# A chunked state-space scan: each step handed to the order of the program in three pieces instead of two

## The chip, the cores and the metric

The kernel runs on one core of a Trainium2 chip. The metric is the device time of one execution in microseconds (us), lower is better. The engines are named as in the profile: PE (TensorE, matrix products), PEld (its weight loads), DVE (VectorE), ACT (ScalarE), POOL (GpSimd) and SP (SyncE, which issues most DMAs). Each engine works through its own instructions strictly in order, and semaphores make it wait for others.

## The reference, cut to what matters

One layer of a streaming encoder for 16 meta tokens and 512 frames, width 1024. The token mixer has two branches, both scans over chunks of 64 frames; a second part (PEER) chooses experts for each token and costs most of the time. The change lies in the second scan, of the SSD branch. Its 32 heads form four groups of eight; the chunk step of the reference, for all groups, is:

```python
def ssd_chunk_step(S, inp):
    xdt, a, Bc, Cc = inp
    acum = jnp.cumsum(a, axis=1)
    seg = jnp.exp(-jnp.abs(acum[:, :, None] - acum[:, None, :]))
    cb = jnp.einsum('btgn,bsgn->btsg', Cc, Bc)
    y = jnp.einsum('btsgr,btsg,bsgrp->btgrp', seg, cb, xdt)
    y = y + jnp.einsum('btgn,bgrpn,btgr->btgrp', Cc, S, jnp.exp(acum))
    to_end = jnp.exp(acum[:, -1:] - acum)
    S = S * jnp.exp(acum[:, -1])[..., None, None] + jnp.einsum('bsgn,bsgr,bsgrp->bgrpn', Bc, to_end, xdt)
    return S, y
```

After the scan y is gated with silu(z), normalised by group, and goes into an up projection. x, B, C and z come from projections of the normed input; x, B and C also pass a convolution over time of four taps.

## The kernel before, in words

The scan is done group by group (0 to 3) by the generator `sscan(g)` (lines 339 to 452). One step i (0 to 3) covers 128 frames, that is two chunks, whose states are sA (before the first) and sB (between the two). A `yield` in a generator gives control back to `drive` (line 53), which has several generators run in turn: it always lets the one run next that is least far on by the weight it was given.

Beside the scan of group g runs `sproj(g+1)`, the projections of the next group, in ten units: two for B and C (`conv`: 48 matmuls into pa and pb, copies rw on ACT, three taps cv on DVE, a silu that ends in BT or CT), four for x (the same, ending in xT, with the transposes px and pxm of an earlier block in two of them and in the two units that follow), and four for z (24 matmuls into pk each). Beside the scan of group 3 run ten units of `gates` (24 matmuls into pq each, then gr), six more gates units follow it, and `lows` (tiles zr, zh), which is placed by the scheduler as early as the scan of group 0. Each unit's weights come by a DMA from SP (raw), are rounded on ACT (whi) and the remainder is formed on DVE (wlo).

After a prologue, a step of the scan has two pieces:

- the pointwise piece: DVE multiplies sgm (the decays between frames) by cb; POOL forms xw, the decayed state sB, sgm times dt, the spread R of the step after (lines 379 to 384), and xd;
- the product piece: ACT normalises the y of the step before; PE does the chunk sums ssp for both states, the diagonal products py from sgm, the transposes pyt of the step before; DVE adds ssp to sB, and py to xd. Then PE does C with the states, pi (lines 435 and 436: the first half of the rows from sA, the second from sB), DVE makes y from pi, xd and z, ACT squares and sums it (into xd and sy), POOL makes ry, and `decays` (lines 386 to 394) starts sgm of the next step: two matmuls pr, a subtraction on DVE, two ACT passes (abs and exp).

The generators give the program order alone. What stands in each engine's queue is decided by a scheduler on top of it, by priority and free buffers, so an instruction can stand earlier than its piece (xw and xd of steps 0 and 1, R of step 2 and later do). The buffers that matter: two of xd, xw and R, three of y and of the weights' raw, whi and wlo, four PSUM banks that ssp, py, pyt, pi, pr, px and pxm share.

Of the kernel before, what the change touches and what calls it, by code (L numbers as in the profile page):

```python
# [40 lines left out]
NGT = 6  # L41
# [15 lines left out]
def drive(*parts):  # L57

    live = [[0, n, g] for n, g in parts]
    while live:  # L60
        p = min(live, key=lambda x: (x[0] + 1) / x[1])
        p[0] += 1
        if next(p[2], StopIteration) is StopIteration:
            live.remove(p)
# [12 lines left out]
def body(tc, a, out):  # L77
# [3 lines left out]
    def act(o, i, f, **kw):  # L81
        S.activation(out=o, in_=i, func=f, **kw)  # L82
# [9 lines left out]
    with ExitStack() as top:  # L92
# [9 lines left out]
        def mps(name):  # L102
            return ps.tile([128, 512], F32, name=name, tag="m")
# [91 lines left out]
        def hv(x, c):  # L195
            return x.rearrange("p (h c) -> p h c", c=c)

        with ExitStack() as mix:
# [140 lines left out]
            def sscan(g):  # L339
# [30 lines left out]
                def turn(i, y):  # L370
                    p = mps("pyt")
                    for h in range(4):
                        T.transpose(p[:, 128 * h:128 * h + 128], y[:, 128 * h:128 * h + 128], ident)
                    yt = sg.tile([128, 512], F32, name="yt", bufs=2)
                    act(yt, p, AF.Copy)
                    nc.sync.dma_start(yT_d[:, 4 * g:4 * g + 4, 128 * i:128 * i + 128], hv(yt, 128))
# [30 lines left out]
                for i in range(TT):  # L407
                    s8 = hv(sgm, 64)
                    tt(V, s8, s8, cb[:, i][:, None, :].to_broadcast([128, 8, 64]), OP.mult)
                    xw = sg.tile([128, 512], F32, name="xw", bufs=2)  # L410
                    tt(G, hv(xw, 64), hv(xs[:, i], 64), bc(tdt[:, i + 1], g), OP.mult)
                    sB = decay(ex[:, i, 64:96], sA)
                    tt(G, s8, s8, bc(dt[:, i + 1], g), OP.mult)
                    if i < 3:
                        R = spread(i + 1)
                    xd = sg.tile([128, 512], F32, name="xd", bufs=2)
                    tt(G, hv(xd, 64), hv(xs[:, i], 64), bc(dsk, g), OP.mult)
                    yield
                    if yp:
                        norm(*yp[1:])  # L420
                    pB = spsum(bt[:, i], xw, slice(0, 64))
                    pA = spsum(bt[:, i], xw, slice(64, 128)) if i < 3 else None
                    tt(V, sB, sB, pB, OP.add)
                    py = mps("py")
                    for h in range(8):
                        cs = slice(64 * h, 64 * h + 64)
                        for c in range(2):
                            rw = slice(64 * c, 64 * c + 64)
                            T.matmul(py[rw, cs], sgm[rw, cs], xs[rw, i, cs], start=True, stop=True)
                    tt(V, xd, xd, py, OP.add)  # L430
                    if yp:
                        turn(*yp[:2])
                    t0 = NM + 128 * i
                    pi = mps("pi")
                    T.matmul(pi[0:64], CT[:, t0:t0 + 64], sA, start=True, stop=True)
                    T.matmul(pi[64:128], CT[:, t0 + 64:t0 + 128], sB, start=True, stop=True)
                    if i < 3:
                        sA = decay(ex[:, i, 96:128], sB)
                        tt(V, sA, sA, pA, OP.add)
                    y = sg.tile([128, 512], F32, name="y", bufs=3)  # L440
                    tt(V, hv(y, 64), hv(pi, 64), bc(ex[:, i], g), OP.mult)
                    tt(V, y, y, xd, OP.add)
                    tt(V, y, y, zt[:, i], OP.mult)
                    sy = sg.tile([128, 1], F32, name="sy")
                    act(xd, y, AF.Square, accum_out=sy)
                    if i < 3:
                        sgm = decays(i + 1, R)
                    yp = (i, y, rstd(sg, sy, 1, 512, "ry", 4 * EPS))
                    yield
# [3 lines left out]
            def gates(n0, n1, pool, nb):  # L453
                for b in range(n0, n1):
                    (p, _, _), = tproj(a["wgate"][b], 1)
                    gr = pool.tile([128, 512], F32, name="gr", tag="t", bufs=nb)
                    act(gr, p, AF.Tanh, scale=0.5)
                    nc.sync.dma_start(ga_d[:, b], gr)
                    yield
# [256 lines left out]
            sg = mix3.enter_context(tc.tile_pool(name="sg", bufs=3))  # L716
# [6 lines left out]
            for g in range(3):  # L723
                s_ = sscan(g)
                next(s_)
                drive((9, s_), (10, sproj(g + 1)))
            s_ = sscan(3)
            next(s_)
            drive((9, s_), (16 - NGT, gates(0, 16 - NGT, sg, 2)),
                  (2 * (NQ + NL - NE) + 5, lows(NE, NQ + NL, lambda n: sg.tile([128, 512], F32, name="zr", bufs=5),  # L730
                                                lambda n: sg.tile([128, 512], F32R, name="zh", bufs=3), S)))
            mix3.close()
# [505 lines left out]
```

## Time and profile before

| | us |
|---|---|
| three runs, median (lowest to highest) | 2148.63 (2145.14 to 2150.17) |
| the profiled execution, its own time | 2149.09 |
| its span, first to last instruction | 2147.3 |
| PE busy | 2071.9 |
| DVE busy | 1537.4 |
| ACT busy | 919.7 |
| POOL busy | 594.0 |

The second scan lies between 330 and 662 us. Groups 0 to 3 begin at 330.5, 417.2, 501.2 and 585.0 us, where the products pcb of each stand. A matmul's end is modelled in these records, so the distance from start to start says more than its duration; a wait that the page puts down to a releaser stands in square brackets.

### The profile page before, as it was taken

To read this page: it belongs to the slowest core of one execution; us is meant where nothing else is said; L and a number is where in the kernel's file an instruction comes from. 1 tells how busy PE (TensorE), PEld (TensorE's weight loads), DVE (VectorE), ACT (ScalarE), POOL (GpSimd) and SP (SyncE) were. 2 spreads that over 40 slices of the span, in tenths; PEclk is the share of its full clock that TensorE was granted. 3 is DMA by queue.
4 is the path that set the end of the run, shared out by engine and by line. 5 is a ranking of instruction groups with operands and counts; after the bars stand their busy time and mean duration, and the time that the engine had idled before them with its cause. 6 is when DMAs were issued, how large, how long until landed. Compare 5 with 4: busy or idle time off the path is not lost.

```text
span 2147.3 us, 33001 instructions
## 1 busy us (share of the span) xinstructions
PE 2071.9 (96%) x12458; PEld 1824.6 (85%) x12458; DVE 1537.4 (72%) x2695; ACT 919.7 (43%) x1468; POOL 594.0 (28%) x536
## 2 busy tenths in 40 slices
PE   5999999999999999989998999999999999999998
PEld 4787777877777989979997989899899989898997
DVE  6543568576653668988998666777777687777776
ACT  6642345554434454444465433333333333333332
POOL 5430224344340000000000004443434444334432
PEclk9899999999999999999999999999999999999999
DMA  8842235222236787679565898899889888988884
GB/s 291 301 163 69 75 106 169 75 69 79 89 104 221 256 269 240 232 260 321 198 247 230 316 295 281 300 316 310 304 311 320 278 325 307 324 301 309 302 303 182
DMA packets 200223, 507.16 MB, mean 236 GB/s; under 512 B 16720, under 2 KB 89040, under 8 KB 198400
## 3 DMA queue, kind: packets, MB, share of 16 engines
q1 hardware_dynamic: 149440, 312.10, 43.1%
q0 software_dynamic: 46592, 185.62, 23.9%
q10 hardware_dynamic: 4032, 7.34, 1.0%
q8 instruction: 97, 1.59, 0.3%
q14 instruction: 62, 0.51, 0.1%
HBM read 448.38 MB, written 56.62 MB: 235 GB/s over the span
## 4 chain that ended last, share of the span: by engine, by line
PE 79%; DVE 7%; issue 5%; DMA 4%; ACT 4%; POOL 1%; SPq 0%; POOLq 0%; ACTq 0%; DVEq 0%
PE va L1111 24%; PE pA L88 7%; PE pA L90 7%; PE pA L89 7%; PE pk L90 3%; PE pk L88 3%; PE pk L89 3%; PE pya L88 2%; PE pya L89 2%; PE pq L254 2%; PE pya L90 2%; PE pq L255 2%; PE pq L257 2%; DVE cv L293 1%; ACT whi L82 1%
## 5 line engine op out<-in xcount | busy, mean ns | idle before, releaser
L82 ACT ACTIVATE whi<-raw 128x1024 fp32r<-128x1024 f32 x433 | 458.4, 1059 | 552.0 <-PE pA L89 297.2
L85 DVE TENSOR_TENSOR wlo<-raw,whi 128x1024 fp32r<-128x1024 f32 x385 | 473.1, 1230 | 202.6 <-ACT whi L82 200.0
L88 PE MATMUL pA<-hh,whi 128*128 128x384 f32 x1024 | 348.4, 340 | 6.8 <-ACT ga L970 4.8
L90 PE MATMUL pA<-hh,wlo 128*128 128x384 f32 x1024 | 347.3, 339 | 1.9 <-DVE wlo L85 1.9
L89 PE MATMUL pA<-hl,whi 128*128 128x384 f32 x1024 | 346.6, 339 | 0.0
L1050 POOL DMA_INDIRECT u<-in_pu,ix x128 | 175.0, 1367 | 323.9 <-ACT gh L1098 279.8
L1050 POOL DMA_INDIRECT u<-in_pv,ix x128 | 168.4, 1315 | 255.9 <-ACT gh L1098 210.0
L1111 PE MATMUL va<-whi,gh 128*128 128x512 f32 x768 | 237.6, 391 | 0.3 <-ACT whi L82 0.3
L1111 PE MATMUL va<-wlo,gh 128*128 128x512 f32 x768 | 237.1, 390 | 0.5 <-DVE wlo L85 0.5
L1064 DVE SCALAR_TENSOR_TENSOR hacc<-u,acg,hacc 128x1024 f32<-128x1024 f32 x128 | 164.5, 1285 | 98.2 <-DMA u<-in_pv,ix 97.3
L1058 DVE SCALAR_TENSOR_TENSOR scr<-u,hg 128x1024 f32<-128x1024 f32 x128 | 156.6, 1223 | 109.1 <-DMA u<-in_pu,ix 108.8
L88 PEld LDWEIGHTS pA<-hh,whi 128*128 128x128 f32 x1024 | 193.4, 189 | 10.9 <-ACT ga L970 5.1
L89 PEld LDWEIGHTS pA<-hl,whi 128*128 128x128 f32 x1024 | 193.9, 189 | 4.1
L1098 ACT ACTIVATE gh<-ga 128x384 fp32r<-128x384 f32 x128 | 67.1, 525 | 303.8 <-PE va L1111 286.2
L90 PEld LDWEIGHTS pA<-hh,wlo 128*128 128x128 f32 x1024 | 193.2, 189 | 2.7 <-DVE wlo L85 2.6
L1111 PEld LDWEIGHTS va<-wlo,gh 128*128 128x128 f32 x768 | 144.2, 188 | 31.5 <-DVE wlo L85 1.0
L1111 PEld LDWEIGHTS va<-whi,gh 128*128 128x128 f32 x768 | 142.8, 188 | 23.1 <-ACT whi L82 0.6
L88 PE MATMUL pya<-oyh,whi 128*128 128x256 f32 x384 | 107.7, 280 | 1.0 <-ACT whi L82 1.0
L89 PE MATMUL pya<-oyl,whi 128*128 128x256 f32 x384 | 107.4, 280 | 0.0
L90 PE MATMUL pya<-oyh,wlo 128*128 128x256 f32 x384 | 107.3, 279 | 0.0
L88 PE MATMUL pk<-whi,hh 128*128 128x512 f32 x256 | 103.0, 402 | 0.0
L90 PE MATMUL pk<-whi,hl 128*128 128x512 f32 x256 | 101.7, 397 | 0.0
(925 smaller groups left out, 4469.1 us busy)
## 6 DMA issues: line engine op xcount, KB each, us to landing
raw<-in_puT SPq DMA_DIRECT2D x128, 512.0 KB, 5.0
raw<-in_pv SPq DMA_DIRECT2D x128, 512.0 KB, 5.3
raw<-in_wup SPq DMA_DIRECT2D x48, 512.0 KB, 4.3
wlo<-lo_d SPq DMA_DIRECT2D x48, 512.0 KB, 4.9
W_d<-stg POOLq DMA_DIRECT2D x12, 2048.0 KB, 9.1
wb<-W_d SPq DMA_DIRECT2D x32, 768.0 KB, 7.7
raw<-in_wpq SPq DMA_DIRECT2D x32, 512.0 KB, 5.4
raw<-in_wxbc SPq DMA_DIRECT2D x24, 512.0 KB, 3.4
```

The lines of the kernel that those rows point to most:

```text
L82: S.activation(out=o, in_=i, func=f, **kw)
L85: eng.tensor_tensor(o, x, y, op=op)
L88: T.matmul(o, lh, rh, start=first, stop=False)
L89: T.matmul(o, lh, rl, start=False, stop=False)
L90: T.matmul(o, ll, rh, start=False, stop=last)
L254: T.matmul(p[:, :n], h[:, k], hh[:, k, sl], start=k == 0, stop=False)
L255: T.matmul(p[:, :n], h[:, k], hl[:, k, sl], start=False, stop=False)
L1050: g_ = G.indirect_dma_start(out=u, out_offset=None, in_=a[tab], in_offset=bass.IndirectOffsetOnAxis(ap=ix[:, i, k:k + 1], axis=0))
L1058: V.scalar_tensor_tensor(scr, u, 1.0, hg[:, i], op0=OP.mult, op1=OP.mult, accum_out=ac_[:, k:k + 1])
L1064: V.scalar_tensor_tensor(hacc[:, i], u, ac_[:, k:k + 1], hacc[:, i], op0=OP.mult, op1=OP.add)
L1098: i = S.activation(out=gh, in_=ga, func=AF.Copy)
L1111: T.matmul(va[t][c], x[:, cs], y[:, 512 * c:512 * c + 512], start=st_, stop=en_)
```

## The change

The product piece gets a `yield` of its own between the transposes of the step before and the product of C with the states. So a step has three pieces, called A (pointwise), B (states and diagonal products) and C (the product with C and all that follows from it), and the weight of the scan in `drive` goes from 9 to 13 turns.

```diff
                     tt(V, xd, xd, py, OP.add)
                     if yp:
                         turn(*yp[:2])
+                    yield
                     t0 = NM + 128 * i
                     pi = mps("pi")
...
                 s_ = sscan(g)
                 next(s_)
-                drive((9, s_), (10, sproj(g + 1)))
+                drive((13, s_), (10, sproj(g + 1)))
             s_ = sscan(3)
             next(s_)
-            drive((9, s_), (16 - NGT, gates(0, 16 - NGT, sg, 2)),
+            drive((13, s_), (16 - NGT, gates(0, 16 - NGT, sg, 2)),
```

By the rule of `drive`, with pK for the K-th projection unit: before, p1 A0 p2 B0 C0 p3 A1 p4 B1 C1 p5 A2 p6 B2 C2 p7 A3 p8 B3 C3 p9 end p10. After, A0 p1 B0 p2 C0 p3 A1 B1 p4 C1 p5 A2 p6 B2 C2 p7 A3 p8 B3 p9 C3 end p10. No instruction is added or taken away.

PE's queue in group 1, from the decays of step 0 (pr) to C of step 1, before; the names carry buffer numbers, sgm_3665 and pi_3841 are of step 0, sgm_3856 and pi_4046 of step 1. Left out are 84 and 96 matmuls of the projection, and the second ssp and the first rows of pi and pr, which stand beside those shown:

```order
L388 MATMUL pr_3662<-R_3655,bdr_2600 128x512
...
L362 MATMUL ssp_3818<-xw_3740,bt_3647 128x512
...
L429 MATMUL py_3823<-xs_2991,sgm_3665 64x64 x16
...
L436 MATMUL pi_3841<-sS_3742,CT_2798 64x512
...
L388 MATMUL pr_3853<-R_3745,bdr_2600 128x512
...
L362 MATMUL ssp_4015<-xw_3935,bt_3647 128x512
...
L429 MATMUL py_4020<-xs_2991,sgm_3856 64x64 x16
L373 MATMUL pyt_4038<-c_cst0_79,y_3847 128x128 x4
...
L436 MATMUL pi_4046<-sS_3937,CT_2798 64x512
```

The same stretch of PE's queue in the change (its lines are one higher from line 433 on); left out are 35, 48, 48, 12 and 36 matmuls, and the same neighbours:

```order
L388 MATMUL pr_3662<-R_3655,bdr_2600 128x512
...
L362 MATMUL ssp_3750<-xw_3670,bt_3647 128x512
...
L429 MATMUL py_3755<-xs_2991,sgm_3665 64x64 x16
...
L437 MATMUL pi_3841<-sS_3672,CT_2809 64x512
...
L388 MATMUL pr_3853<-R_3675,bdr_2600 128x512
...
L362 MATMUL ssp_3946<-xw_3935,bt_3647 128x512
...
L429 MATMUL py_3951<-xs_2991,sgm_3856 64x64 x16
L373 MATMUL pyt_3969<-c_cst0_79,y_3847 128x128 x4
...
L437 MATMUL pi_4046<-sS_3937,CT_2809 64x512
```

B0 and B1 have moved one unit of 48 matmuls ahead, and C0 and C1 stand where they stood. Group 2 has the same order; in group 0 no matmuls stand between ssp and py of step 1, and in group 3 neither (its units have 24 matmuls, and 16 stand between pr and ssp of step 0). Step 2 is in its old place in one piece in all groups. In step 3, C stands one unit later than before.

POOL's queue in group 1, from xw of step 2 to the state that step 2 starts from, before (sgm_3856 is of step 1, ry_3860 of step 0, xw_4147 and xd_4155 of step 2, xw_4334 and R_4152 of step 3, sS_4049 is the state):

```order
L85 TENSOR_TENSOR xw_4147<-xs_2991,tdt_111 128x512
L85 TENSOR_TENSOR sS_3844<-sS_3742,ex_110 128x512
L85 TENSOR_TENSOR R_4152<-c_cst1_96,ath_2598 128x512
L85 TENSOR_TENSOR R_4152<-c_cst1_96,atl_2599 128x512
L85 TENSOR_TENSOR sS_3937<-sS_3844,ex_110 128x512
L85 TENSOR_TENSOR sgm_3856<-sgm_3856,dt_107 128x512
L85 TENSOR_TENSOR ry_3860<-ry_3860,mhalf_81 128x1
L85 TENSOR_TENSOR xd_4155<-xs_2991,dsk_112 128x512
L85 TENSOR_TENSOR xw_4334<-xs_2991,tdt_111 128x512
L85 TENSOR_TENSOR sS_4049<-sS_3937,ex_110 128x512
```

And in the change:

```order
L85 TENSOR_TENSOR xw_4147<-xs_2991,tdt_111 128x512
L85 TENSOR_TENSOR sS_3844<-sS_3672,ex_110 128x512
L85 TENSOR_TENSOR sS_3937<-sS_3844,ex_110 128x512
L85 TENSOR_TENSOR R_4152<-c_cst1_96,ath_2598 128x512
L85 TENSOR_TENSOR R_4152<-c_cst1_96,atl_2599 128x512
L85 TENSOR_TENSOR xd_4155<-xs_2991,dsk_112 128x512
L85 TENSOR_TENSOR ry_3860<-ry_3860,mhalf_81 128x1
L85 TENSOR_TENSOR sS_4049<-sS_3937,ex_110 128x512
L85 TENSOR_TENSOR xw_4334<-xs_2991,tdt_111 128x512
L85 TENSOR_TENSOR sgm_3856<-sgm_3856,dt_107 128x512
```

The last factor of sgm of step 1, on which py of step 1 waits, has gone from directly behind the state to behind xd, ry, the next state and xw. In group 0 it stands behind xd and ahead of ry; in group 3 it has kept its place.

DVE's queue in group 1, from the y of step 0 to the product of sgm of step 1 with cb, before:

```order
L85 TENSOR_TENSOR y_3847<-pi_3841,ex_110 128x512
L85 TENSOR_TENSOR sgm_3856<-pr_3853,ac_109 128x512
L283 SCALAR_TENSOR_TENSOR CT_3670<-silu_t_3815,cv_3810 128x528
L85 TENSOR_TENSOR y_3847<-y_3847,xd_3748 128x512
L287 MEMSET rw_3946 128x3
L85 TENSOR_TENSOR y_3847<-y_3847,zt_3426 128x512
L85 TENSOR_TENSOR sgm_3856<-sgm_3856,cb_3640 128x512
```

And in the change, from the weight split ahead of it; of the three taps cv the first is shown, the others stand at the next two gaps, a memset at the third:

```order
L85 TENSOR_TENSOR wlo_4083<-raw_4080,whi_4082 128x1024
L85 TENSOR_TENSOR y_3847<-pi_3841,ex_110 128x512
L293 SCALAR_TENSOR_TENSOR cv_3833<-rw_3773,c_cst1_96,cv_3833 128x528
L85 TENSOR_TENSOR y_3847<-y_3847,xd_3678 128x512
...
L85 TENSOR_TENSOR y_3847<-y_3847,zt_3426 128x512
...
L85 TENSOR_TENSOR sgm_3856<-pr_3853,ac_109 128x512
L180 TENSOR_SCALAR ry_3860<-sy_3851 128x1
...
L283 SCALAR_TENSOR_TENSOR CT_3681<-silu_t_3838,cv_3833 128x528
L85 TENSOR_TENSOR sS_3937<-sS_3937,ssp_3946 128x512
L85 TENSOR_TENSOR sgm_3856<-sgm_3856,cb_3640 128x512
```

The subtraction that starts sgm of step 1 has gone behind the whole of y and the three taps of the convolution. On ACT the normalising pass of y of step 0 now stands between the two passes over sgm of step 1, in groups 1 and 2. On SP the stores of yt move by one or two places against the loads of weights. At the end of group 3, the last transposes pyt stand one matmul ahead of the end of their gates unit, where they stood one unit earlier, and on ACT the copy yt stands directly ahead of the gates' copy gr.

## Rows read from the trace of the kernel before

**Rows 1.** The page's busy times of the engines, with their share of the span and their instructions.

```profile
PE 2071.9 (96%) x12458; PEld 1824.6 (85%) x12458; DVE 1537.4 (72%) x2695; ACT 919.7 (43%) x1468; POOL 594.0 (28%) x536
```

**Rows 2.** Busy time in the four groups of the scan: stretch, its length, busy us of PE, PEld, DVE, ACT and POOL (with instructions), granted share of TensorE's clock, DMA share, GB/s.

```profile
330.50:417.20 86.70, 82.80 (x610) 68.04 (x609) 65.47 (x88) 45.39 (x82) 38.32 (x31) 0.96 0.36 118
417.20:501.20 84.00, 80.78 (x612) 65.83 (x611) 58.53 (x80) 41.73 (x75) 35.86 (x31) 1.00 0.25 76
501.20:585.00 83.80, 80.57 (x610) 65.75 (x609) 58.45 (x78) 41.51 (x75) 35.86 (x31) 1.00 0.25 76
585.00:662.00 77.00, 76.71 (x446) 55.48 (x445) 36.89 (x48) 30.84 (x51) 23.60 (x23) 1.00 0.34 113
```

**Rows 3.** What PE waited for between 325 and 655 us: total us, times, longest us.

```profile
PE pi L435 <- DVE sS L85: 8.9, 5, 3.1
PE px L314 <- DVE xd L85: 0.7, 1, 0.7
```

**Rows 4.** PE in order of time, group 0: start us, us, instruction, and in brackets the wait ahead of it with its releaser. The rows are: the first ssp of step 0, the first pr of the decays behind it, the first pyt and the first waiting pi of step 1, the first ssp of step 2.

```profile
345.31 1.13 PE L362 MATMUL ssp<-xw,bt 64*128 64x512 f32 x4
...
348.45 0.50 PE L387 MATMUL pr<-R,bdr 128*128 128x512 f32 x1
...
362.97 0.66 PE L373 MATMUL pyt<-c_cst,y 128*128 128x128 f32 x4
366.73 0.64 PE L435 MATMUL pi<-sS,CT 128*64 128x512 f32 x1 [3.10 <-DVE sS L85]
...
384.89 1.13 PE L362 MATMUL ssp<-xw,bt 64*128 64x512 f32 x4
```

**Rows 5.** The same for group 1, steps 0 to 2 (ssp and the two pr of step 0, ssp, pi and a transpose behind step 1, ssp and pi of step 2). Between the second pr and the ssp that follows stand 96 matmuls of the projection.

```profile
432.04 1.13 PE L362 MATMUL ssp<-xw,bt 64*128 64x512 f32 x4
...
435.88 0.50 PE L387 MATMUL pr<-R,bdr 128*128 128x512 f32 x1
436.21 0.39 PE L388 MATMUL pr<-R,bdr 128*128 128x512 f32 x1
...
448.25 1.13 PE L362 MATMUL ssp<-xw,bt 64*128 64x512 f32 x4
...
452.61 0.64 PE L435 MATMUL pi<-sS,CT 128*64 128x512 f32 x1 [1.57 <-DVE sS L85]
...
455.36 0.28 PE L317 MATMUL pxm<-c_cst,xT 128*16 128x128 f32 x1 [0.20 <-DVE sS L85]
...
467.49 1.13 PE L362 MATMUL ssp<-xw,bt 64*128 64x512 f32 x4
...
471.63 0.64 PE L435 MATMUL pi<-sS,CT 128*64 128x512 f32 x1 [1.35 <-DVE sS L85]
```

**Rows 6.** Stretches in which the granted clock was at its lower level, and one in which it was not (columns as in rows 2).

```profile
313.40:316.80 3.40, 3.40 (x10) 2.61 (x9) 3.40 (x4) 1.61 (x4) 3.01 (x2) 0.50 0.56 180
368.00:374.80 6.80, 6.12 (x26) 5.38 (x26) 6.77 (x10) 2.47 (x6) 4.01 (x3) 0.50 0.41 116
452.60:662.00 209.40, 204.22 (x1364) 157.94 (x1364) 127.20 (x171) 94.47 (x164) 79.54 (x72) 1.00 0.29 92
1060.90:1064.30 3.40, 3.40 (x13) 3.40 (x14) 2.82 (x8) 0.55 (x2) 0.00 (x0) 0.50 0.54 178
```

**Rows 7.** PE's waits of the whole run, three of them: total us, times, longest us. The one for xT ended at 312.4 us, the one for xf at 1060.8 us, the one for gr at 663.2 us.

```profile
PE psc L1004 <- DVE xf L1001: 2.5, 1, 2.5
...
PE px L314 <- DVE xT L283: 2.3, 1, 2.3
...
PE pq L254 <- ACT gr L82: 1.4, 1, 1.4
```

**Rows 8.** Groups of instructions of POOL, DVE and ACT in group 1 (417.2 to 501.2 us): line, engine, operation, tiles, shapes, count, busy us, mean ns of one, idle time ahead of them with its releasers.

```profile
L85 POOL TENSOR_TENSOR sS<-sS,ex 128x512 f32<-128x512 f32 x7 | 8.7, 1240 | 10.2 <-DVE sS L85 10.2
L85 POOL TENSOR_TENSOR xw<-xs,tdt 128x512 f32<-128x512 f32 x4 | 5.8, 1450 | 12.6 <-PE ssp L362 10.3 <-ACT xs L82 2.3
...
L85 POOL TENSOR_TENSOR xd<-xs,dsk 128x512 f32<-128x512 f32 x4 | 5.3, 1316 | 4.6 <-ACT xd L82 4.6
...
L85 POOL TENSOR_TENSOR sgm<-sgm,dt 128x512 f32<-128x512 f32 x4 | 4.2, 1044 | 8.4 <-DVE sgm L85 8.4
L85 POOL TENSOR_TENSOR ry<-ry,mhalf 128x1 f32<-128x1 f32 x4 | 2.2, 548 | 0.0
...
L293 DVE SCALAR_TENSOR_TENSOR cv<-rw,c_cst,cv 128x528 f32<-128x528 f32 x18 | 15.1, 839 | 1.7 <-ACT cv L82 1.5
L85 DVE TENSOR_TENSOR wlo<-raw,whi 128x1024 fp32r<-128x1024 f32 x10 | 13.0, 1304 | 13.7 <-ACT whi L82 13.7
L85 DVE TENSOR_TENSOR sS<-sS,ssp 128x512 f32<-128x512 f32 x7 | 4.7, 678 | 1.3 <-PE ssp L362 1.3
...
...
L82 ACT ACTIVATE whi<-raw 128x1024 fp32r<-128x1024 f32 x10 | 10.5, 1051 | 5.2 <-PE pk L90 2.7 <-PE pb L255 2.5
L82 ACT ACTIVATE sgm<-sgm 128x512 f32<-128x512 f32 x8 | 5.1, 633 | 2.6 <-DVE sgm L85 2.4
...
L82 ACT ACTIVATE y<-y,ry 128x512 f32<-128x512 f32 x4 | 2.9, 723 | 4.7 <-POOL ry L85 4.7
```

**Rows 9.** The chain from pr to the finished sgm of step 0 in group 1, in order of time: its first link on DVE and its last on POOL.

```profile
421.86 0.69 DVE L85 TENSOR_TENSOR sgm<-pr,ac 128x512 f32<-128x512 f32 x1 [0.21 <-PE pr L388]
...
425.60 1.04 POOL L85 TENSOR_TENSOR sgm<-sgm,dt 128x512 f32<-128x512 f32 x1 [0.63 <-DVE sgm L85]
```

## The prediction

> **What bounds the kernel now.** I read the busy line of the page first: PE works 2071.9 of 2147.3 us, 96%, and the next engine, DVE, 72% [rows 1]. Then the windows of the four scan groups: PE is busy for 82.80 of 86.70, 80.78 of 84.00, 80.57 of 83.80 and 76.71 of 77.00 us, and DVE for 65 us or less of each [rows 2]. So the scan is bound by PE's queue, and every microsecond in which PE does not stand should come off the end. PE's waits say where it stands: five waits of pi for the state sS, 8.9 us together, the longest 3.1, and one of a transpose px for xd, 0.7 [rows 3]. In order of time, group 0 has one wait of 3.10, ahead of C1 (pi of step 1, 366.73) [rows 4]; group 1 has 1.57 and, behind it, 0.20 at C1, and 1.35 at C2 [rows 5]; group 2 repeats group 1 (8.9 - 3.10 - 1.57 - 1.35 leaves 2.9).
>
> The clock adds to this. Behind the 3.10 us the granted clock is 0.50 from 368.0 to 374.8, while it is 1.00 from 452.6 on, behind the waits of 1.57 and 1.35 [rows 6]. Elsewhere a stretch of 3.4 us at 0.50, the 1.2 GHz level, follows the wait of 2.3 that ended at 312.4 and the one of 2.5 that ended at 1060.8 [rows 6, 7]. So in these rows a stand of 1.57 costs itself alone, and one of 2.3 and over costs half of a 3.4- or 6.8-us stretch on top, 1.7 or 3.4 us. The distance from C1 to ssp of step 2 bears that out: 18.16 us in group 0 (384.89 - 366.73), 14.88 in group 1 (467.49 - 452.61), 3.28 more [rows 4, 5].
>
> **The change part by part.** No instruction comes or goes. B0 and B1 move a unit of 48 matmuls earlier; in these groups 96 matmuls and one pr take 12.04 us (436.21 to 448.25) [rows 5], so a unit is 6.0.
>
> What it removes. The wait at C1 comes from the chain sS: ssp, a DVE add, pi at once behind it. With a unit between, 6.0 us of PE work cover the 1.1 of ssp and the 0.68 of the add [rows 5, 8], so the C1 waits go. Group 0 gets back 3.10 + 3.3 of slow clock = 6.4. Groups 1 and 2 get back 1.57 + 0.20, and at C0 the difference in the way from ssp to pr, 3.84 in group 1 against 3.14 in group 0 (435.88 - 432.04, 348.45 - 345.31), 0.70 [rows 4, 5]: 2.5 each. Step 2 stays in one piece, so its 1.35 stays too, unless PE is slow or late just ahead of it. Group 3 has 0.29 idle by its window and the one px wait of 0.7 in the list (the window hides waits inside a modelled matmul) [rows 2, 3]; I take 0.7 as removed.
>
> What it adds, at B0 and B1: py needs sgm, which it now wants 6.0 us earlier. For **B0** the chain is pr, subtraction, two ACT passes, product, POOL: in group 1 from 421.86 to 426.64, 4.8 us, if nothing comes between [rows 9]. A unit of 6.0 us stood between pr of step 0 and B0 and now the chain just fits; 0 to 0.8 us of wait, I take 0.3 in groups 1 and 2, and 0.7 in group 0, whose window is the busiest for DVE (65.47) [rows 2].
>
> **B1 in groups 1 and 2** is the critical term. The order shows three changes around sgm of step 1, each of which I price with group 1's means [rows 8]; time 0 is the start of C0's first pi. On DVE: whi on ACT 1.05 and wlo 1.30 come first, then y, cv, y, cv, y, cv: 3 x 0.68 (priced as the add of sS) and 3 x 0.84, then the subtraction of sgm, 0.68, so 7.6. The last of the three y feeds ACT's square, done at 6.9. ACT: abs of sgm .63 to 8.2; the norm of y (.72) has to wait for ry, and stands ahead of exp: xd of step 2 on POOL waits for the square, 6.9 + 1.32 = 8.2, ry .55 = 8.8, norm 9.5, exp 10.1; the product with cb on DVE 10.8. POOL: the next state waits for ssp (7.4 at PE, 1.2) and the add .68, 9.3, and takes 1.24 to 10.5; xw of step 3 1.45 to 12.0; sgm 1.04 to 13.0. PE: the pi and pr of C0 take 1.0, a unit 6.0, the ssp of step 1 and 12 more matmuls 2.6; it reaches py at about 9.9 (with 0.3 for transposes). **The wait is 3.1 us.** From below: with every POOL pass at 1.04, the fastest of them, it is 13.0 - 0.2 - 0.4 - 9.9 = 2.5, and if DVE's start is a microsecond earlier, as it would be with wlo already done, POOL is still held by ssp. A bound below that is an order of POOL's work in which xw finds its place ahead of the state: then 1.0. From above: each of the three POOL passes at 1.5 and wlo later by 0.5, 3.9. I take 3.1, nearest to the means of the rows.
>
> By the rows a stand of 3.1 drops the clock, for 3.4 or 6.8 us. I take 3.4 us, 1.7 lost, since most stretches read are that long [rows 6]. That slow stretch gives DVE and POOL time, so the 1.35 at C2 goes in this case. Groups 1 and 2 each: 2.5 + 1.35 - 0.3 - 3.1 - 1.7 = **-1.3**.
>
> POOL and DVE share something that shows in the same rows: POOL's 128x512 pass takes 1.04 us for sgm and 1.24 to 1.45 for sS, xd and xw, which run beside more DVE work [rows 8]. The Trainium skill, "Trainium Architecture — The Big Picture", section "What this means for kernel authors", says that VectorE and GpSimd contend for a port pair, by an exclusive lock and not by a division of the bandwidth. Were that taken at its word, a POOL pass would wait out one DVE pass of 0.68 us and take 1.72, and the three passes ahead of py would put its wait at some 4 us and not 3.1; no row of group 1 has a mean that long.
>
> **Group 0:** sgm of step 1 stands on POOL behind xd of step 2 alone, and its subtraction on DVE directly behind the first y. By the same prices xd is done at some 6.6 us after C0's first pi and sgm at 7.6, and PE reaches py at 8.1 (1.0 + 6.0 + 1.1); the wait is taken as 0. C2's wait, which the slow clock hid before, may come back: 0 to 1.35, I take 0.5. Net 6.4 - 0.7 - 0.5 = **+5.2**. **Group 3:** keeps its POOL place; 0.7 saved, 0.5 for py of its half-size units (24 matmuls, 3.0 us, against a chain of 4.8, but 16 of them stand further on): **+0.2**.
>
> **End of the stage.** C3 one unit later brings pyt(3) to the end of the gates unit, and the copy yt ahead of gr on ACT. PE waited 1.4 for gr at 663.2 [rows 7]; a copy more makes it 1.9: **-0.5**, and -2.2 if the clock falls as after 2.3. In groups 0 to 2 the last y has a unit less before its group ends, but the next group's prologue does not read it, and DVE and POOL have room: 0. The yt stores of SP move by one or two places against the loads of weights; there are three raw buffers and what PE waits for in the scan is DVE's sS and xd [rows 3], so 0; without that cover, some tenths per unit.
>
> Sum: 5.2 - 2 x 1.3 + 0.2 - 0.5 = **2.3 us** less than the profiled execution's 2149.09. That lies 0.5 above the median of 2148.63 of the runs shown, so I set the forecast at 2148.63 - 2.3, about **2146.5**. A measurement of this kernel tells 0.2%, 4.3 us, from no change; this forecast is inside.
>
> **The rivals.** *POOL makes it in time* (faster). If the scheduler's late place of sgm holds PE for 1.0 only, it is under 1.57, the clock stays at 1.00, and C2's 1.35 is back: groups 1 and 2 give 2.5 - 0.3 - 1.0 = +1.2 each, total 5.2 + 2.4 + 0.2 - 0.5 = 7.3, **2141.3**. For it: POOL is busy 35.86 of 84.00 us [rows 2], so it has slack. Against: the xw and state passes in front are chained to PE's ssp, not to POOL's load. It decides below about 1.6 us of wait. 0.25.
>
> *The late py drops the clock for long* (slower). B1's wait in groups 1 and 2 reaches 3.9 and takes the 6.8-us stretch that group 0 shows behind 3.10 [rows 4, 6]: 3.85 - 0.3 - 3.9 - 3.4 = -3.8 each, and the gate's 1.9 falls too, -2.2: 5.2 - 7.6 + 0.2 - 2.2 = -4.4, **2153.0**. The place is POOL's queue, xd to sgm; it decides when the wait plus its slow clock passes 6.0 us in each group (3.85 - 0.3 - 6.0 = -2.45, twice that eats the 4.9 of the others), so from a wait of 2.6 with the long stretch. For it: the only wait over 3 us in the scan took the long one. Against: two of the three stretches read were short. 0.16.
>
> *The gain is given back later:* the stages behind the scan end when they did, since some transfer or a slower engine sets their start: **2148.6**. For it: little; the waits that the list of the whole run shows are for DVE and ACT [rows 7]. 0.07. That the change does not do what it says is seen in part: step 2 stays whole, and the scheduler places 12 matmuls ahead of py. That is in the sum.
>
> **How the numbers follow.** Forecast 0.52, faster rival 0.25, slower rival 0.16, no effect 0.07. The forecast's own range is 2144 to 2150 (group 0 from 4 to 6, groups 1 and 2 from 0 to -2.5 each). The faster rival puts most of its chance below 2144.3, the slower one a little over half above 2152.9; the forecast case gives 0.03 to each side. So faster 0.25, within 0.2% 0.62, slower 0.13. The range reaches to the rivals' own values: 2141 to 2153.
>
> **What would show it.** Right: no wait of pi for sS at step 1 in any group and granted clock 1.00 where group 0 had 0.50; a new wait of py for POOL's sgm at step 1 of groups 1 and 2, 2.5 to 3.9 us, with a stretch at 0.50 behind it; pq waiting for gr by about 1.9. The sum is wrong if py of step 1 waits under 1.6 us (then faster), if the stretch at 0.50 lasts 6.8 us (then slower), or if py of step 0 waits over 1 us in all groups, which would mean that a unit of 6.0 us does not cover the 4.8-us chain of sgm.

## The result

The change is slower: 2156.72 us median of six runs (2155.14 to 2158.98) against 2146.89 (2143.74 to 2150.17), ratio 1.0051, 95% interval 1.0039 to 1.0063, some 10 us. The prediction had 2146.5.

The profiled execution took 2158.98 us, 9.9 more than that of before. PE is busy no longer than before (answers [rows 1]); it stands still for longer:

```profile
PE 2068.3 (96%) x12458; PEld 1819.5 (84%) x12458; DVE 1541.9 (71%) x2695; ACT 916.8 (43%) x1468; POOL 605.0 (28%) x536
```

The windows of the four scan groups, from one pcb to the next and to the wait for gr, answer to [rows 2] (columns as there):

```profile
331.45:418.67 87.22, 80.73 (x611) 65.44 (x610) 66.58 (x88) 44.24 (x82) 40.15 (x31) 1.00 0.35 114
418.67:507.94 89.27, 82.19 (x610) 67.17 (x609) 60.91 (x81) 40.86 (x75) 37.57 (x31) 0.98 0.23 72
507.94:597.19 89.25, 82.10 (x610) 67.06 (x609) 60.84 (x79) 40.85 (x75) 37.59 (x31) 0.98 0.22 72
597.19:674.78 77.59, 76.23 (x446) 54.83 (x445) 37.85 (x49) 31.95 (x52) 24.65 (x23) 1.00 0.35 112
```

Cut at the same places, the groups of before took 86.7, 83.9, 83.9 and 78.1. So groups 1 and 2 lose 5.4 us each, group 0 loses 0.5 where I expected 5.2 less, group 3 gains 0.5: 10.7 in all, against 9.9 for the whole execution, so the loss lies in the scan. What PE waits for in the scan (325 to 680 us; total, times, longest) answers to [rows 3]:

```profile
PE py L429 <- POOL sgm L85: 9.1, 4, 3.8
PE px L314 <- DVE xT L283: 5.1, 3, 2.0
PE pyt L373 <- ACT y L82: 3.3, 4, 1.1
PE pi L436 <- DVE sS L85: 3.0, 3, 1.0
PE pq L254 <- ACT gr L82: 1.2, 1, 1.2
```

The state of C1 is waited for no more; the 3.0 that are left are C2. In its place stand three kinds of wait (py, px and pyt), of which I had priced the first only. In order of time, group 1 on PE (answers [rows 5]):

```profile
443.25 1.13 PE L362 MATMUL ssp<-xw,bt 64*128 64x512 f32 x4
...
449.81 1.15 PE L429 MATMUL py<-xs,sgm 64*64 64x64 f32 x32 [3.77 <-POOL sgm L85]
...
467.09 0.66 PE L314 MATMUL px<-c_cst,xT 128*128 128x128 f32 x4 [1.52 <-DVE xT L283]
...
477.43 0.64 PE L436 MATMUL pi<-sS,CT 128*64 128x512 f32 x1 [0.98 <-DVE sS L85]
```

And the end of group 0, the last transposes, with the same wait of 0.72 at the ends of groups 1 and 2:

```profile
418.08 0.66 PE L373 MATMUL pyt<-c_cst,y 128*128 128x128 f32 x4 [0.72 <-ACT y L82]
```

Behind the late py the clock falls, and where group 0 had its slow stretch it is whole in this execution (two windows, columns as in rows 2, answers [rows 6]):

```profile
451.20:454.50 3.30, 3.30 (x18) 3.30 (x17) 2.62 (x6) 1.24 (x2) 0.00 (x0) 0.50 0.71 232
360.00:367.00 7.00, 6.03 (x50) 6.03 (x51) 6.96 (x10) 3.95 (x7) 3.35 (x3) 1.00 0.60 201
```

It need not be: f_fill_wait (below), whose edit leaves group 0 as it is in the change, has a slow stretch behind its py and pyt there, and its group 0 takes 88.0 us:

```profile
358.90:362.30 3.40, 3.36 (x16) 3.37 (x17) 3.37 (x4) 3.21 (x6) 2.17 (x2) 0.53 0.61 224
```

Who held sgm? DVE in order of time, from C0 (its pi starts at 435.74, its second pr at 437.09):

```profile
436.70 1.23 DVE L85 TENSOR_TENSOR wlo<-raw,whi 128x1024 fp32r<-128x1024 f32 x1 [1.33 <-ACT whi L82]
437.84 0.68 DVE L85 TENSOR_TENSOR y<-pi,ex 128x512 f32<-128x512 f32 x1
438.44 0.95 DVE L293 SCALAR_TENSOR_TENSOR cv<-rw,c_cst,cv 128x528 f32<-128x528 f32 x1
439.31 1.54 DVE L85 TENSOR_TENSOR y<-y,xd 128x512 f32<-128x512 f32 x1
440.78 1.55 DVE L293 SCALAR_TENSOR_TENSOR cv<-rw,c_cst,cv 128x528 f32<-128x528 f32 x1
...
443.53 0.68 DVE L85 TENSOR_TENSOR sgm<-pr,ac 128x512 f32<-128x512 f32 x1
...
447.08 1.55 DVE L85 TENSOR_TENSOR sgm<-sgm,cb 128x512 f32<-128x512 f32 x1 [1.12 <-ACT sgm L82]
```

ACT and POOL over the same stretch:

```profile
444.24 0.63 ACT L82 ACTIVATE sgm<-sgm 128x512 f32<-128x512 f32 x1
445.81 0.72 ACT L82 ACTIVATE y<-y,ry 128x512 f32<-128x512 f32 x1 [0.93 <-POOL ry L85]
446.44 0.61 ACT L82 ACTIVATE sgm<-sgm 128x512 f32<-128x512 f32 x1
```

```profile
447.05 1.04 POOL L85 TENSOR_TENSOR xw<-xs,tdt 128x512 f32<-128x512 f32 x1
448.71 1.04 POOL L85 TENSOR_TENSOR sgm<-sgm,dt 128x512 f32<-128x512 f32 x1 [0.62 <-DVE sgm L85]
```

The subtraction starts 6.4 us behind the second pr; the same one in the kernel before started 2.95 us behind its pr of 436.21 [rows 5]:

```profile
439.16 0.67 DVE L85 TENSOR_TENSOR sgm<-pr,ac 128x512 f32<-128x512 f32 x1
```

That is 3.5 us more, nearly as much as py waits. Then exp stands behind the norm of y, which waits for ry. The order of POOL's queue is not what holds it last: xw is done at 448.1, and POOL then stands 0.62 us for DVE's product. But the product itself takes 1.55 us beside xw, 0.87 more than y or the subtraction; the last section comes back to that.

### The profile page after: what moved, and what is told of

Its sections match the earlier page's. It is cut to its first block, busy times and chain, and to the rows that moved or that the text cites. A ratio compares the mean times of both kernels' runs of the same rounds, so it can differ in the third digit from the quotient of the medians.

```text
span 2157.2 us, 33011 instructions
## 1 busy us (share of the span) xinstructions
PE 2068.3 (96%) x12458; PEld 1819.5 (84%) x12458; DVE 1541.9 (71%) x2695; ACT 916.8 (43%) x1468; POOL 605.0 (28%) x536
## 4 chain that ended last, share of the span: by engine, by line
PE 75%; DVE 9%; DMA 5%; issue 5%; ACT 4%; POOL 2%; SPq 0%; ACTq 0%; POOLq 0%; DVEq 0%
PE va L1112 24%; PE pA L88 7%; PE pA L89 7%; PE pA L90 7%; PE pk L90 2%; PE pk L88 2%; PE pk L89 2%; DVE wlo L85 2%; PE pq L254 2%; PE pq L255 2%; ACT whi L82 2%; PE pq L257 2%; PE pya L88 1%; PE pya L89 1%; PE pya L90 1%
```

## The experiments

In all kernels of this section the pieces A, B and C are turns of their own, and the order of the turns is written out as a string (s a piece of the scan, p a projection unit), in which a move is one letter in another place. Their line numbers are 17 or more higher. The lengths of the groups (us, of the profiled execution, cut as above) and the ratio to before with its interval:

| run | group 0 | 1 | 2 | 3 | ratio |
|---|---|---|---|---|---|
| before | 86.7 | 83.9 | 83.9 | 78.1 | 1 |
| the change | 87.2 | 89.3 | 89.3 | 77.6 | 1.0051 (1.0039 to 1.0063) |
| s1_only_step1 | 88.6 | 84.2 | 84.3 | 78.0 | 1.0018 (1.0009 to 1.0027) |
| s0_only_step0 | 87.4 | 85.2 | 85.2 | 77.6 | 1.0020 (1.0011 to 1.0029) |
| s3_only_step3 | 85.9 | 84.8 | 84.9 | 78.1 | 1.0015 (1.0005 to 1.0025) |
| v_sgm_dve | 87.4 | 89.0 | 88.9 | 77.9 | 1.0055 (1.0042 to 1.0068) |
| d_decays_in_b | 86.8 | 84.1 | 84.1 | 79.3 | 1.0007 (0.9998 to 1.0016) |
| d_decays_first_in_c | 89.1 | 89.1 | 89.0 | 78.8 | 1.0056 (1.0043 to 1.0069) |
| f_fill_wait | 88.0 | 88.3 | 88.4 | 77.6 | 1.0063 (1.0048 to 1.0077) |
| n_apart | 88.8 | 86.0 | 84.5 | 79.8 | 1.0031 (1.0019 to 1.0042) |
| n_apart_late_px | 88.2 | 86.7 | 87.6 | 79.8 | 1.0030 (1.0021 to 1.0039) |
| b_ssp_early | 87.2 | 83.4 | 83.4 | 77.9 | 1.0010 (1.0000 to 1.0020) |
| b_states_early | 87.5 | 83.4 | 83.4 | 77.9 | 1.0009 (0.9999 to 1.0019) |
| a_mid_px | 88.6 | 91.7 | 91.7 | 77.6 | 1.0072 (1.0058 to 1.0085) |
| d_mid_px | 86.4 | 85.2 | 85.3 | 79.3 | 1.0003 (0.9994 to 1.0012) |
| b_mid_px | 84.5 | 83.3 | 83.3 | 78.1 | 0.9963 (0.9950 to 0.9977) |
| b_ssp_mid | 84.8 | 81.0 | 81.1 | 77.9 | 0.9952 (0.9938 to 0.9965) |

Two cautions: the scan began anywhere from 326.9 to 332.1 us in executions with the same code ahead of it, so I compare lengths and waits, not the hour; and the slow stretch in group 0 is 3.4 us long in some executions and 6.8 or missing in others, so that a difference of a microsecond or two in group 0 alone says little.

**Which of the three moves costs.**

```diff
-woven("spspspsspspspsspspspssp", s_, sproj(g + 1))   # the change
+woven("pspsspsspspspsspspsspsp", s_, sproj(g + 1))   # s1: B1 alone early
+woven("spspspspsspspsspspsspsp", s_, sproj(g + 1))   # s0: B0 alone early
+woven("pspsspspsspspsspspspssp", s_, sproj(g + 1))   # s3: C3 alone late
```

> Only the states and diagonal products of step 1 go one projection unit earlier; steps 0 and 3 are as before. In the profile of the change, groups 1 and 2 lost 5.4 us each, 3.8 of it in one wait of py for sgm at step 1. Theory DVE: that wait arises because the product of C in step 0 stands alone behind a unit, so that y and the subtraction of sgm meet the unit's weight split and its taps on DVE; with step 0 in its old place its sgm is ready about 7.6 us after pr, as before, against 7.1 us of PE work, and py of step 1 waits 0.3 to 0.8. The waits of C1 for the state go (3.1 and its slow clock in group 0, 1.6 in groups 1 and 2), and a wait of px for xT of 1.5 to 2 comes in each of groups 0 to 2, since a unit and C alone (8 us) do not cover the chain of a convolution (9.6): the scan 2 to 4 us shorter than before, ratio about 0.9985. Theory step: moving step 1 earlier is what costs, wherever step 0 stands: py waits 3 us or more and the ratio is about 1.005.

> Only the states and diagonal products of step 0 go one unit earlier. Theory DVE: sgm of step 1 is as late as in the change (its subtraction 6 us behind pr in groups 1 and 2), but nobody waits for it, since its product stands two units on; the wait of C1 for the state is back (1.6, and about 3 with slow clock in group 0); ratio 0.999 to 1.001. Theory step: early step 0 costs by itself, py of step 0 waits over 1 us in all groups, ratio above 1.002.

> Only the product of C in step 3, and the last transposes with it, go one unit later. If the 0.72 us that the last pyt of groups 0 to 2 waits for ACT's y in the profile of the change comes from this move: three such waits, 2.2 us in all, and about 0.2 at the end, ratio 1.001. If it comes from the other moves: no such waits and ratio 1.000.

Measured, of s1 and of s0, what PE waits for in the scan:

```profile
PE py L446 <- POOL sgm L102: 5.1, 3, 3.7
PE px L331 <- DVE xT L300: 4.6, 3, 1.5
PE pi L453 <- DVE sS L102: 3.0, 3, 1.0
```

```profile
PE pi L453 <- DVE sS L102: 11.5, 3, 4.5
PE py L446 <- POOL sgm L102: 0.6, 1, 0.6
```

s1: in groups 1 and 2 py of step 1 waits 0.7, as expected of theory DVE, and with step 0 in its old place the groups lose 0.3; the wait of px for xT is there, 1.5 in each of groups 0 to 2. In group 0, though, py waits 3.67 and the clock falls (0.50 from 359.7 to 363.2), which I had not expected: group 0 takes 88.6 us and not less than 86.7, and the ratio is 1.0018 and not the 0.9985 of that theory. So the late py of groups 1 and 2 takes two moves, step 0 (which makes sgm late) and step 1 (which asks for it early); either alone does not make it. s0: C1's wait did not come back at 1.6 but at 3.5 (4.5 in group 0), and the ratio, 1.0020, is above the range of theory DVE. DVE of s0 ahead of it, where pi stood until 454.18:

```profile
451.69 1.22 DVE L102 TENSOR_TENSOR wlo<-raw,whi 128x1024 fp32r<-128x1024 f32 x1
452.83 0.70 DVE L300 SCALAR_TENSOR_TENSOR xT<-silu_t,cv 128x528 f32<-128x528 f32 x1
453.45 0.68 DVE L102 TENSOR_TENSOR sS<-sS,ssp 128x512 f32<-128x512 f32 x1
```

The add of the state stands behind work of a unit that has come late itself. s3: three waits of pyt for y, 0.72 each, as expected, and groups 1 and 2 are 0.95 longer. The ratios of the three add up to 1.0053, as if they were independent; the groups show that they are not (1.3, 0.3 and 0.95 in group 1 against 5.4 together), so that sum is partly chance.

**What holds sgm: POOL's order or the start on DVE.**

```diff
-tt(G, s8, s8, bc(dt[:, i + 1], g), OP.mult)
+tt(V if i == 1 else G, s8, s8, bc(dt[:, i + 1], g), OP.mult)    # v_sgm_dve
...
+if i < 3: nsg = decays(i + 1, R)    # d_decays_in_b: ahead of the yield between B and C
 yield
+if i < 3: nsg = decays(i + 1, R)    # or d_decays_first_in_c: here, ahead of pi
 pi = mps("pi")
...
-sgm = decays(i + 1, R)
+sgm = nsg
```

> The change as it is, but the last factor of sgm of step 1 is taken on DVE and not on POOL, so that POOL's order holds it no more. Theory POOL (the one of the prediction: xd, ry, the state and xw stand ahead of sgm): sgm is done with DVE's product with cb, py of step 1 waits 1.1 us or less in groups 1 and 2 and the clock stays at 1.00: about 8 us less than the change. Theory DVE (the subtraction starts 6.1 us behind pr, behind the weight split, y and the taps): the wait falls by one pass only, to about 2.7, and the scan gains 1 us a group or less.

> The change, with the decays of the next step (pr and what follows) taken out of C and put at the end of B, so that sgm of the next step is started one projection unit sooner, ahead of y on DVE. Theory DVE (the late start of sgm behind y and the taps is what py waits for): the wait of py at step 1, 3.8 us in groups 1 and 2 and 0.9 in group 0, is gone and with it the half clock; groups 1 and 2 fall from 89.3 to about 84.0 us each, group 0 by 1 to 2. The waits of px for xT (1.5 to 2.0), of C2 for the state (1.0) and of the last pyt for y (0.7) stay, so that the whole is about the kernel before: ratio 0.998 to 1.001. Rival: DVE is full in these stretches, and what py no longer waits comes back as a longer wait of pi or px: groups 1 and 2 stay above 87 us, ratio above 1.003.

> The change, with the decays of the next step placed ahead of pi inside C: PE does pr a microsecond sooner, and the subtraction of sgm comes ahead of y and two of the three taps on DVE; everything else is in its place. Theory DVE: sgm is finished about 3 us sooner, py of step 1 waits 0.5 to 1.9 us in groups 1 and 2, groups 1 and 2 fall by 2 to 4.5 us each, ratio 1.001 to 1.003. Rival: the chain is held elsewhere (ACT's normalising pass between abs and exp, the product with cb): the wait stays above 3 us and the ratio at 1.005.

v_sgm_dve: with the last factor taken out of POOL's queue py still waits 3.46 in groups 1 and 2 and the ratio stays at 1.0055. Theory POOL, the one of my prediction, had 1.1 or less and is out as the main cause. Theory DVE had 2.7; DVE takes the next state (0.67) ahead of the factor, and the product still takes 1.55 beside xw, so this run does not take all of POOL's part away. d_decays_in_b: py of step 1 no longer waits, and groups 1 and 2 are 84.06 and 84.07 where 84.0 was expected; the ratio is that of before within its interval. So the late sgm costs these two groups 5.2 us each: with its whole chain a unit sooner they are back at the length of before, and what C1 gives is eaten by px, pyt and pr. Its windows of groups 1 and 2:

```profile
416.54:500.60 84.06, 80.50 (x610) 65.60 (x610) 58.69 (x81) 40.30 (x75) 39.67 (x31) 1.00 0.25 76
500.60:584.67 84.07, 80.50 (x610) 65.62 (x609) 58.63 (x79) 40.30 (x75) 39.67 (x31) 1.00 0.25 76
```

d_decays_first_in_c missed: the subtraction began 0.4 us behind the second pr, 6 us sooner than in the change, and the wait of py fell to 2.0, but the last two passes over sgm came late now (the product with cb behind y and the taps, 443.11, and POOL's behind xd, 444.65), the clock still fell (0.98 in group 1, as in the change), pyt waited 1.1 and at step 2 pr, which stands ahead of pi here, 1.4, and nothing was gained. A start 6 us sooner helps only where each later pass has its place too.

**What the wait costs beside itself.**

```diff
 py = mps("py")
+if i == 1 and g in (1, 2):
+    for _ in range(5):
+        T.matmul(py, bt[:, i], xw, start=True, stop=True)
```

> The change with five matmuls more ahead of py of step 1 in groups 1 and 2, whose result py overwrites: work that fills PE's wait for sgm and ends before it. They add nothing to the chain that py waits for. If the wait itself is all that the late sgm costs, the groups take as long as in the change (89.3 us). If the half clock behind the wait is a cost of its own, it goes: granted clock 1.00 in groups 1 and 2 and each 1.4 to 1.8 us shorter than the change; ratio about 1.0035.

The wait of py is 0.09 and the granted clock 1.00. Six microseconds from py on, of the change and of f_fill_wait:

```profile
449.80:455.80 6.00, 5.99 (x60) 5.93 (x61) 4.52 (x7) 1.24 (x2) 0.00 (x0) 0.72 0.41 134
```

```profile
447.80:453.80 6.00, 6.00 (x73) 5.93 (x74) 5.28 (x7) 1.43 (x3) 1.91 (x1) 1.00 0.29 90
```

At 0.72 of the clock 1.7 us of 6.0 are lost, and 60 matmuls are begun against 73. The groups are 0.9 shorter and not 1.4 to 1.8, since the 12 matmuls of the unit that the change has ahead of py now stand behind it (1.5 us more) while sgm came 0.8 sooner (POOL took it ahead of xw, and DVE's product, with no xw beside it, took 0.69). That the slow clock costs time of its own is shown by the two windows, its share of a group only by this sum. The ratio, 1.0063 from four runs, does not show these 0.9.

**A unit between all of them.**

```diff
+woven("spspsspspsspspsspspspsp", s_, sproj(g + 1))   # n_apart, with the decays at the end of B
...
-if b >= XLAG: turn(b - XLAG, x_[b - XLAG])    # n_apart_late_px, too: px behind
 ... the unit's matmuls ...
+if b >= XLAG: turn(b - XLAG, x_[b - XLAG])
```

> The decays at the end of B, and in every step a unit between B and C: A0 p1 B0 p2 C0 A1 p3 B1 p4 C1 A2 p5 B2 p6 C2 A3 p7 B3 p8 C3 p9 end p10. Every wait of pi for the state is covered by a unit. Theory unit (each chain needs one unit of PE work between its two ends, and sgm, sS and xT all have it now but xT, whose 9.6 us chain has a unit and one piece, 8 us): px waits 1 to 1.5 us for xT in two places of each group, the last pyt 0.7 no more (a unit stands ahead of it), groups 1 and 2 take 82 to 83.5 us against 83.9 before; ratio 0.996 to 0.999. Rival (DVE and ACT are what bounds these stretches): new waits of 2 to 4 us, ratio above 1.001.

> The same as n_apart, and the transposes px and pxm of a block stand behind the matmuls of their unit and not ahead of them, so that the chain of xT has two units. Theory unit: the waits of px go too, groups 1 and 2 take about 81.5 us, group 0 83 to 84, group 3 77; 8 to 10 us less than the kernel before, ratio 0.9955 to 0.997. Rival (DVE and ACT bound): ratio no lower than n_apart's.

Both went the rival's way, 1.003: pr waited up to 2.15 until DVE's add of the state was done, pyt up to 1.6; with px late, py 3.7 in step 2 of groups 1 and 2, for ACT's xs. pr reads nothing of the state, so its wait is, by the code, one for the PSUM bank that ssp holds until the add. A unit for every chain is not enough; whether the banks or the rows of ACT and DVE set these waits was not separated. The same wait of 2.15 dropped the granted clock in group 1 of n_apart (0.51 from 468.6 to 472.0) and not in group 2 (1.00 from 554.5 to 561.0), so here the length of one stand does not tell whether the clock falls.

**The state alone, and what swallowed its gain.**

```diff
 tt(G, hv(xd, 64), hv(xs[:, i], 64), bc(dsk, g), OP.mult)
+pB = spsum(bt[:, i], xw, slice(0, 64))      # b_ssp_early, turns as before:
+pA = ...                                     # out of B, ahead of its unit
+tt(V, sB, sB, pB, OP.add)                    # (b_states_early: the next sA, too)
 yield
```

> The kernel before, with its two pieces, in which only the sums ssp and the add of sB are moved out of the product piece to the end of the pointwise piece, one unit earlier; py, the transposes, pi and the decays stay in their places. What the change was after (a unit between ssp and pi) without moving sgm's reader py or the pieces of C. Theory place (the change lost because py and C moved, so that sgm and xT lost their cover; ssp alone has nothing behind it that is late): the waits of pi for the state at C1 and C2 are gone, no new wait of py or px over 0.5 us, group 0 about 81 to 83 us, groups 1 and 2 about 81 each, ratio 0.9945 to 0.997. Rival (any unit between ssp and pi upsets DVE and ACT enough to give it back): new waits of 2 us or more a group, ratio 0.999 or above.

> As b_ssp_early, and the whole state that the next step starts from (its decay on POOL and its add on DVE) is also formed in the pointwise piece. By theory place the same ratio within 0.1%, with the remaining wait at C, if any, smaller, since the add of the second state no longer stands beside y. By the rival ratio 0.999 or above.

All waits for the state are gone in both, but groups 1 and 2 are only 0.5 shorter, group 0 is 0.5 longer or more, and the ratios, 1.0010 and 1.0009, are the rival's: PE now stands at px, behind pr. ACT of b_ssp_early up to what releases it, and PE:

```profile
447.87 1.04 ACT L99 ACTIVATE whi<-raw 128x1024 fp32r<-128x1024 f32 x1
...
449.50 0.83 ACT L99 ACTIVATE cv<-rw,c_cst 128x528 f32<-128x528 f32 x1
450.23 0.58 ACT L99 ACTIVATE yt<-pyt 128x512 f32<-128x512 f32 x1
```

```profile
450.86 0.65 PE L331 MATMUL px<-c_cst,xT 128*128 128x128 f32 x4 [1.61 <-ACT yt L99]
```

px needs none of yt's data, so by the code the wait is for a bank: py, pyt, pi and pr share four, and px gets one when ACT has copied pyt out, behind the weights and copies of the unit. The fifth user of four banks gave the gain back; in group 0 this one wait is 5.6 us.

**px in the middle of its unit.**

```diff
 for k in range(KC):
+    if k == 4 and mid:
+        mid.pop()()
...
-turn(b - XLAG, x_[b - XLAG])
+mid.append(lambda b=b: turn(b - XLAG, x_[b - XLAG]))
```

In units of z the same stands in the middle of a unit's 24 matmuls. It was put into the change (a_mid_px), into d_decays_in_b (d_mid_px), into before (b_mid_px) and into b_ssp_early (b_ssp_mid).

> The change, with the transposes px and pxm of a block placed in the middle of their projection unit and not ahead of it; all else, the late py of step 1 too, stays. Theory of two terms (py's late sgm and its clock, and px's xT, add up): the waits of px for xT (2.05 in group 0, 1.5 in groups 1 and 2) go, the wait of py of 3.8 stays, groups 1 and 2 take about 87.7 us, group 0 about 85; ratio about 1.003. Rival: the waits of px are only the place where a late PSUM bank or ACT shows; they come back at pi or py, ratio 1.005.

> d_decays_in_b (the change, with the decays at the end of B) with px and pxm in the middle of their unit. The waits of px for xT (1.28 and 1.15) go; 0.4 at C2 and 0.7 at the last pyt stay: groups 1 and 2 about 81.7 us, ratio 0.997 to 0.9985. Rival as for b_ssp_mid: ratio 1.000 or above.

> b_ssp_early (ssp and the add of the state one unit early, all else as in the kernel before) with px and pxm in the middle of their unit. If what took the place of C's waits there was the bank that px needed right behind pyt, pi and pr (1.6 and 1.1 us in groups 1 and 2, 5.6 in group 0), and half a unit covers ACT's copy yt: no wait over 0.5 us is left in the groups, group 0 about 80.5, groups 1 and 2 about 80.8 us, ratio 0.9935 to 0.996, faster than both kernels. Rival (DVE and ACT bound the groups, whatever PE's order): other waits of 1 us or more a group, ratio 0.999 or above.

> The kernel before, with px and pxm in the middle of their unit and nothing else changed; it tells what of b_ssp_mid (ratio 0.9952) is due to this edit alone. Theory of two edits: the waits of C1 and C2 for the state (3.1, 1.57, 1.35) have nothing to do with px and stay; only the wait of px at 312 us, ahead of the scan, goes with its slow clock; the groups take within 0.7 us of before and the ratio is 0.997 to 0.9995. Rival (px's place alone gives the gain): groups 1 and 2 at 81.5 us or less, ratio 0.9955 or lower.

a_mid_px: the rival. px waits no more, but C2 waits 2.8 for its state and the clock falls there; groups 1 and 2 get 2.4 us longer (in group 1 the slow stretch behind py is longer, too). So px's 1.5 was no term that adds to the others: it was cover for C2, whose wait grew by 1.8. d_mid_px the same: 2.76 at pr of step 2, no gain. b_mid_px: groups 1 and 2 within 0.6 of before, as expected; the ratio of 0.9963 is a little better than my range, over half of it outside the scan (the wait of 2.3 at 312 us [rows 7] is 0.3, and its slow stretch is gone) and 2.2 us in group 0. b_ssp_mid: groups 1 and 2 have no wait left:

```profile
410.43:491.44 81.01, 81.01 (x611) 66.10 (x610) 58.10 (x80) 40.25 (x75) 36.83 (x31) 1.00 0.25 79
491.44:572.49 81.05, 81.05 (x611) 66.11 (x611) 58.04 (x78) 40.25 (x75) 36.83 (x31) 1.00 0.25 79
```

81.0 us, all of it PE's own work, against 83.3 with px moved alone and 83.4 with ssp moved alone: the early ssp is worth 2.3 us a group once px is out of its way, and 0.5 without. In group 0 one wait of 2.7 for a bank is left, and it takes 84.8 us and not the 80.5 expected. b_ssp_mid is faster than both kernels, 2133.12 us median of five runs, 0.5% below before, and by the two ratios about 1% below the change. Most of that is px's place alone: the interval of b_mid_px (0.9963) overlaps its own, and only the lengths of groups 1 and 2 tell the two apart.

## Why the prediction was wrong

By its own steps:

- **What bounds the kernel** was right: PE's queue, and the waits of the scan decide. One row was read at the wrong place: the px wait of 0.7 for xd [rows 3] lies at 370.2 in group 0, inside its slow stretch, and not in group 3. It is part of the 3.28 that I took for the slow clock of group 0, so the sum counts it twice.
- **The waits at C1 go**: right in all groups; so does C0's 0.70 (from its first pi to pr 1.01 us, 1.70 before).
- **B1 in groups 1 and 2**, 3.1 us and 1.7 of clock: 3.8 and 1.7 measured. The size was near, in part by chance; the carrier was not. I had POOL's order as the holder; v_sgm_dve shows that it is not the main one, and d_decays_in_b that the lateness of the chain from pr on is. Both were in my sum, counted from C0's first pi (435.74 here): DVE's product done at 10.8 us, POOL's xw at 12.0, so that POOL came last. Measured were 12.9 and 12.4: the subtraction began at 7.8 and not 6.9, exp waited behind a norm that waited for ry, and the product took 1.55 beside POOL's xw and not 0.68. That 0.87 is POOL's part in the wait, by the passes side by side and not by the order that I had priced.
- **"That slow stretch gives DVE and POOL time, so the 1.35 at C2 goes"**: wrong. C2 waits 0.98 and 0.09 behind it, more than 20 us after the stretch.
- **What I did not price**, and here the step failed that decided the sign: that a product piece is cover for other chains. A unit's own chain (weights, copies, taps, xT, px) takes 9.6 us behind the unit's end (457.4 to 467.0 in group 1). Before, a piece B with C and a unit stood between, and px found xT 2.3 us early. With B gone from there, C and a unit are shorter than the chain: px waits 1.5 to 2.05. The xT and its px before, and the xT of the change:

```profile
457.30 1.36 DVE L283 SCALAR_TENSOR_TENSOR xT<-silu_t,cv 128x528 f32<-128x528 f32 x1
460.98 0.60 PE L314 MATMUL px<-c_cst,xT 128*128 128x128 f32 x4
```

```profile
465.98 1.05 DVE L283 SCALAR_TENSOR_TENSOR xT<-silu_t,cv 128x528 f32<-128x528 f32 x1
```

Likewise y, ahead of the last pyt: "a unit less ... 0" was 0.72 three times. Together 2.2 us in each of groups 1 and 2, on top of C2's 1.1. Over the scan px and pyt wait 5.1 and 3.3 us; the sum had nothing for them, and these 8.4 alone turn its 2.3 saved into 6.1 lost. This tells where PE stood, not what an edit would give back: a_mid_px took the wait of px away and gained nothing.
- **Group 0, +5.2**: -0.5. The 3.1 and the slow stretch went, as said; in their place came py 0.60 and 0.91, pyt 1.10, px 2.05, C2 0.99 and 0.10, the last pyt 0.72: 6.5 us. I had 1.2 for them. These sums leave about half a microsecond open in each of groups 0 to 2.
- **The end of the stage**, -0.5: the wait for gr is 1.21 and not 1.9; group 3 gained 0.5.

The slower rival, 2153.0, had the right wait (py of step 1) but put it down to POOL's queue, and its terms were not the right ones: the clock fell for 3.4 us and not for 6.8, and the rest of the loss was px, C2 and pyt. The range ended at that rival's value because its bounds went up to the worst of one chain only.

## What to carry to other kernels

Where PE's queue binds and a wait is covered by moving a piece, list what the piece itself was covering: every chain that runs through the other engines between two PE instructions, with the PE work that lies between them before and after, and the PSUM banks that are held in between. Taking a wait away brings PE sooner to the next chain; if that was late by less, the gain stops there, as at px in b_ssp_early, and an edit that seems to cost nothing (px in the middle of its unit) is what lets it through. Move the smallest part that the late chain needs, here ssp and its add, and not the piece in which it was written.

## What was not expected of the hardware

I had priced DVE's and POOL's passes each by its own mean. In the pairs below, which stand side by side, the one that begins second waits for the other. In the change POOL's xw begins at 447.05 and takes 1.04 us; DVE's product with cb begins 0.03 behind it, takes 1.55 and ends 0.54 behind the end of xw. In f_fill_wait POOL takes sgm ahead of xw, nothing on POOL runs beside the same product, and it takes 0.69:

```profile
445.92 0.69 DVE L102 TENSOR_TENSOR sgm<-sgm,cb 128x512 f32<-128x512 f32 x1 [1.11 <-ACT sgm L99]
```

```profile
446.69 1.04 POOL L102 TENSOR_TENSOR sgm<-sgm,dt 128x512 f32<-128x512 f32 x1 [0.77 <-DVE sgm L102]
```

Earlier in the change the two take turns: DVE's y (439.31) and cv (440.78) take 1.54 and 1.55 and end 0.55 and 0.57 behind POOL's two passes of R. Not every DVE pass is held: y from pi, which comes from PSUM, takes 0.68 at 437.84, in the middle of POOL's state:

```profile
436.90 1.93 POOL L85 TENSOR_TENSOR sS<-sS,ex 128x512 f32<-128x512 f32 x1 [4.79 <-PE pi L437]
438.79 1.51 POOL L85 TENSOR_TENSOR R<-c_cst,ath 128x512 fp32r<-128x512 f32 x1
440.26 1.50 POOL L85 TENSOR_TENSOR R<-c_cst,atl 128x512 fp32r<-128x512 f32 x1
```

The Trainium skill, "Trainium Architecture — The Big Picture", section "What this means for kernel authors", has the port pair of VectorE and GpSimd as an exclusive lock. The trace agrees: the pass that begins first keeps its length (xw, 1.04), and a DVE pass that begins second ends half a microsecond behind it. In the prediction I had let each POOL pass wait out a whole DVE pass (by its own prices 4.5 us for py, not some 4) and argued against it from means; what decides is which of the two begins first. R beside y and cv put off the start of sgm by 1.65 us (1.54 and 1.55 against the 0.68 of y and the 0.76 of cv with nothing beside them), and xw put off its product by 0.87. f_fill_wait shows the second part, with sgm 0.8 us sooner; no run moves R alone, so what that would give back is not shown.
